# A hybrid attention / mLSTM trunk: the order of its instructions taken from a planner written into the kernel, with its own layout of the PSUM banks

## The chip, the cores and the metric

The kernel runs on one core of a Trainium2 chip. The metric is the device time of one execution in microseconds (us), the median of three runs. The chip's engines are called TensorE (matmuls), VectorE, ScalarE, GpSimd and SyncE here, and PE, DVE, ACT, POOL and SP in the profile; PEld is TensorE's loading of weights.

## The reference

One inference step of a trunk with two layers, for 512 sample tokens and 128 prompt tokens of 1024 features, in float32. Cut to what matters:

```
for l in range(2):
    shift, scale, gate = split(silu(c) @ W_mod[l] + b_mod[l])
    h = rmsnorm(x) * (1 + scale) + shift
    proj = h @ W_in[l]                       # 1024 x 5840
    o_a = latent attention, 4 heads          # low-rank q and kv, a shared rotary key
    o_b = differential attention, 4 heads    # two softmax maps a head, rmsnorm
    o_c = mLSTM, 4 heads, both directions    # gates -> scans -> per-chunk matmuls
    y = concat(o_a * silu(z_a), o_b * silu(z_b), o_c * silu(z_c)) @ W_out[l]
    x = x + gate * y
y_sample, y_prompt = rmsnorm(x) * g_final
```

Outputs are also the caches and the final mLSTM states of the prompt.

## The kernel before

The 640 tokens are five tiles of 128. Every large product is exact to nearly float32: each operand is split into a high and a low part (`hi`, `lo`), and `mm3` (L288 to L290) makes three matmuls of it. A weight section is loaded by SP into one of three `raw` slots, ScalarE casts the high part (L279), VectorE or, for each third section, GpSimd subtracts to get the low part (L282); both go to five slots of `fixr`. `tm_unit` gives token-major projections (tiles `tm`), `fm_unit` feature-major ones (`fm`), `out_proj` and `out_tail` the output projections (`op`), which VectorE multiplies by the gate (L538), GpSimd adds to the residual (L539), and a DMA of the ACT queue writes back (L540).

A layer runs the mLSTM branch (`gates`, then `mlstm_head` four times), differential attention (`diff_head`), latent attention (`mla_prep`, `mla_head`), each a chain of dependent steps. `Feed` holds the independent work (projections, the next layer's modulation) and is asked for a portion of it at each step of a chain, so that the program text already alternates chain and independent work. The Tile framework then orders each engine's instructions by a timeline of its own (`schedule_with_timeline_sim=True`). `issue_after` keeps the first layer's first section behind the modulation weights on SP.

Tiles of PSUM have three tags: `pj` (projections, 2 buffers of one bank), `sm` (small, 3), `S` (two banks each, 2: scores, transposes). The framework gives them banks as they come free, so that a projection may stand in a bank that a transposed tile has just left. Long-lived SBUF tiles share 35 slots of tag `Q`.

Names used below: `ds` scores of differential attention (L921, L922), made from `ksh`/`kp` and `ksl` (the high and low keys, L813 on ScalarE and L816 on VectorE) after the transposes `pkd` (L892); `pa` the transposes of the gate columns (L696), which need `gta` (L678) at the end of the scans `gb`, `edge`, `gta`, `gm` on VectorE; `as` scores of latent attention (L1149); `oT` transposes of a head's output (L513); `po` the product with the values (L831); `xT` transposes of the normalised tokens (L434); `sz` the SiLU of a gate path (L496); `msc`, a DRAM tile through which the row `gm` is spread over the partitions as `mb`.

Of the kernel before, what the change touches and what calls it, by code (L numbers as in the profile page):

```python
# [65 lines left out]
def parameter_columns(I):  # L66
    """Vectors of the inputs laid out as columns of 128, and the gate biases and stabilisers on their gate rows."""
# [12 lines left out]
class Feed:  # L80
    """Independent work, emitted in portions between the steps of a dependent chain."""
# [39 lines left out]

@with_exitstack
def tile_hybrid(ctx: ExitStack, tc: tile.TileContext, I: dict, O: dict):
    nc = tc.nc
    V, A, G, T = nc.vector, nc.scalar, nc.gpsimd, nc.tensor
# [3 lines left out]
    pp = ctx.enter_context(tc.tile_pool(name="pp", bufs=1, space=PSUM))  # L129
    dr = ctx.enter_context(tc.tile_pool(name="dr", bufs=1, space=DRAM))  # L130

    # independent work of a layer, in the order in which it fills the gaps of the dependent chains
# [7 lines left out]
    class Fixed:  # L140
        """One tile from which all that stays in its place is cut."""
# [14 lines left out]
    class Ring:  # L156
        """Slots used in turn, for tiles that live for a short stretch of the program."""
# [14 lines left out]
    def qt(name, dt=F32, n=TOK):  # L172
        return sb.tile([P, 645], dt, tag="Q", bufs=NQ, name=name)[:, 0:n]
# [7 lines left out]
    def pj(name):  # L181
        return pp.tile([P, 512], F32, tag="pj", bufs=2, name=name)

    def sm(name):
        return pp.tile([P, 512], F32, tag="sm", bufs=3, name=name)

    def s2(name):
        return pp.tile([P, 1024], F32, tag="S", bufs=2, name=name)

    # ---------------------------------------------------------------- constants and parameters  # L190
    A.preload_act_table_set("exp_and_others")
    con = fix.tile([P, C_END])
    nc.sync.dma_start(out=con[:, 0:C_RC], in_=I["consts"][:, 0:C_RC])
# [9 lines left out]
    # silu(cond) as stationary columns: [c_hi, ctx_hi, c_lo, ctx_lo] per k  # L203
# [13 lines left out]
    # half conv weights; norm gains with the half of z's silu  # L217
# [7 lines left out]
    def more_params():  # L225
        nc.sync.dma_start(out=con[:, C_RC:], in_=I["consts"][:, C_RC:])
# [6 lines left out]
    def lambdas(l):  # L233
        dl = qt("dl")
        nc.sync.dma_start(out=dl[:, 0:256],
# [11 lines left out]
    # ---------------------------------------------------------------- helpers  # L247
# [125 lines left out]
    def gate_tile(l, hf):  # L373
        """The residual gates of half of the features for the sample and for the prompt, on all partitions."""
        gs = [qt("gate", n=512) for _ in range(2)]
        for w in range(2):
            nc.sync.dma_start(out=gs[w], in_=grow[l][w:w + 1, hf * 512:(hf + 1) * 512].to_broadcast([P, 512]))
# [987 lines left out]
```

## Time and profile before

| | us |
|---|---|
| median of 3 runs | 1403.42 (1402.33 to 1403.47) |
| the profiled execution, first to last instruction (its span) | 1399.6 |
| TensorE matmul busy | 1310.0 (94%) |
| VectorE busy | 842.5 (60%) |
| ScalarE busy | 630.2 (45%) |
| GpSimd busy | 385.5 (28%) |
| DMA, mean rate | 112 GB/s |

The profiled execution is one of its own: its span is 1399.6 us, and what a run takes around the span is in the runs' 1403.42 us but not in it. Busy time of TensorE is that of pipelined matmuls whose ends are modelled, so 94% is not 94% of its peak; it is the time in which it had a matmul in hand.

### The profile page before, as it was taken

To read this page: it belongs to the slowest core of one execution; us is meant where nothing else is said; L and a number is where in the kernel's file an instruction comes from. 1 tells how busy PE (TensorE), PEld (TensorE's weight loads), DVE (VectorE), ACT (ScalarE), POOL (GpSimd) and SP (SyncE) were. 2 spreads that over 40 slices of the span, in tenths; PEclk is the share of its full clock that TensorE was granted. 3 is DMA by queue.
4 is the path that set the end of the run, shared out by engine and by line. 5 is a ranking of instruction groups with operands and counts; after the bars stand their busy time and mean duration, and the time that the engine had idled before them with its cause. 6 is when DMAs were issued, how large, how long until landed. Compare 5 with 4: busy or idle time off the path is not lost.

```text
span 1399.6 us, 24039 instructions
## 1 busy us (share of the span) xinstructions
PE 1310.0 (94%) x9300; PEld 1218.9 (87%) x9300; DVE 842.5 (60%) x1786; ACT 630.2 (45%) x1333; POOL 385.5 (28%) x335
## 2 busy tenths in 40 slices
PE   8989999989899999999979899999999999899995
PEld 3789899969899999798769899998799999878984
DVE  2576757765567465854465767675655646385446
ACT  5454544433455545255365345443343445435433
POOL 0421422323223013511432213333322202161142
PEclk9999999999999999999989999999999999999998
DMA  9423323264223223531751333434521211242154
GB/s 341 116 83 101 111 84 112 85 212 136 81 83 111 61 62 113 167 109 54 238 176 31 84 112 86 117 82 129 180 84 57 74 46 63 87 138 85 54 173 150
DMA packets 164642, 156.40 MB, mean 112 GB/s; under 512 B 14193, under 2 KB 130593, under 8 KB 164529
## 3 DMA queue, kind: packets, MB, share of 16 engines
q1 hardware_dynamic: 154032, 135.92, 32.0%
q10 hardware_dynamic: 10496, 18.95, 3.6%
q8 instruction: 73, 1.20, 0.3%
q14 instruction: 41, 0.33, 0.1%
HBM read 131.38 MB, written 23.46 MB: 111 GB/s over the span
## 4 chain that ended last, share of the span: by engine, by line
PE 73%; DVE 12%; DMA 5%; ACT 4%; issue 2%; POOL 2%; SPq 1%; DVEq 0%; ACTq 0%; POOLq 0%
PE tm L288 8%; PE tm L289 8%; PE tm L290 8%; PE fm L288 6%; PE fm L290 6%; PE fm L289 6%; PE po L831 5%; PE op L288 2%; PE pT L826 2%; PE op L289 2%; PE op L290 2%; DVE fixr L282 1%; PE nd L767 1%; PE ds L921 1%; DVE ksl L816 1%
## 5 line engine op out<-in xcount | busy, mean ns | idle before, releaser
L288 PE MATMUL tm<-fixr 128*128 128x256 f32 (+2 forms) x1040 | 302.0, 291 | 12.4 <-DVE kp L816 4.8
L289 PE MATMUL tm<-fixr 128*128 128x256 f32 (+2 forms) x1040 | 299.4, 288 | 0.2 <-DVE fixr L282 0.2
L290 PE MATMUL tm<-fixr 128*128 128x256 f32 (+2 forms) x1040 | 297.0, 287 | 2.5 <-DVE fixr L427 2.2
L282 POOL TENSOR_TENSOR fixr<-fix,fixr 128x1024 fp32r<-128x1024 f32 (+4 forms) x51 | 121.4, 2380 | 385.0 <-ACT fixr L279 365.4
L279 ACT CAST fixr<-fix 128x1024 fp32r<-128x1024 f32 (+2 forms) x154 | 157.8, 1030 | 128.7 <-PE fm L289 38.4
L288 PEld LDWEIGHTS tm<-fixr 128*128 128x128 f32 x1040 | 201.0, 193 | 15.3 <-issue 4.7
L290 PEld LDWEIGHTS tm<-fixr 128*128 128x128 f32 x1040 | 200.3, 193 | 3.0 <-DVE fixr L427 2.4
L289 PEld LDWEIGHTS tm<-fixr 128*128 128x128 f32 x1040 | 201.0, 193 | 1.4 <-issue 0.9
L288 PE MATMUL fm<-fixr 128*128 128x320 f32 x640 | 201.3, 314 | 0.5 <-ACT od L940 0.5
L290 PE MATMUL fm<-fixr 128*128 128x320 f32 x640 | 199.3, 311 | 0.0
L289 PE MATMUL fm<-fixr 128*128 128x320 f32 x640 | 198.6, 310 | 0.0
L282 DVE TENSOR_TENSOR fixr<-fix,fixr 128x1024 fp32r<-128x1024 f32 (+3 forms) x103 | 141.6, 1377 | 66.8 <-ACT fixr L279 62.3
L288 PEld LDWEIGHTS fm<-fixr 128*128 128x128 f32 x640 | 120.3, 188 | 2.2 <-ACT od L940 0.8
L290 PEld LDWEIGHTS fm<-fixr 128*128 128x128 f32 x640 | 120.2, 188 | 0.9 <-issue 0.9
L289 PEld LDWEIGHTS fm<-fixr 128*128 128x128 f32 x640 | 120.4, 188 | 0.0
L539 POOL TENSOR_TENSOR xp<-xp,ytmp 128x512 f32<-128x512 f32 x60 | 79.1, 1329 | 107.7 <-DVE ytmp L538 58.4
L288 PE MATMUL op<-fixr,oTh 128*128 128x512 f32 x240 | 100.5, 419 | 2.9 <-ACT oTh L516 1.7
L289 PE MATMUL op<-fixr,oTh 128*128 128x512 f32 x240 | 96.7, 403 | 0.0
L290 PE MATMUL op<-fixr,oTl 128*128 128x512 f32 x240 | 95.0, 403 | 0.0
L929 ACT ACTIVATE P<-ds,fix 128x640 f32<-128x640 f32 (+1 forms) x80 | 56.7, 709 | 72.7 <-DVE fix L928 70.4
L927 DVE TENSOR_REDUCE fix<-ds 128x1 f32<-128x640 f32 (+1 forms) x80 | 56.8, 713 | 47.4 <-PE ds L922 31.0
L252 POOL TENSOR_TENSOR fix<-fix 128x5 f32<-128x5 f32 (+1 forms) x31 | 31.6, 1019 | 130.4 <-DVE fix L251 129.9
(325 smaller groups left out, 2722.2 us busy)
## 6 DMA issues: line engine op xcount, KB each, us to landing
fix<-in_W_in SPq DMA_DIRECT2D x56, 512.0 KB, 4.2
fix<-in_W_mod SPq DMA_DIRECT2D x35, 512.0 KB, 4.3
fix<-in_W_in SPq DMA_DIRECT2D x64, 256.0 KB, 3.3
xd<-xp ACTq DMA_DIRECT2D x60, 256.0 KB, 2.5
xp<-xd SPq DMA_DIRECT2D x50, 256.0 KB, 4.4
fix<-in_W_out SPq DMA_DIRECT2D x24, 512.0 KB, 5.0
gate<-grow SPq DMA_DIRECT2D x32, 256.0 KB, 5.0
wm<-in_W_mod SPq DMA_DIRECT2D x26, 256.0 KB, 5.9
```

Of the source, the lines that this page charges most:

```text
L252: G.tensor_tensor(r[:, :n], a[:, :n], mhalf[:, :n], op=ALU.pow)
L279: A.copy(hv, rv)
L282: e.tensor_tensor(lv, rv, hv.bitcast(F32), op=ALU.subtract)
L288: T.matmul(ps, lhsT=wh, rhs=xh, start=start, stop=False)
L289: T.matmul(ps, lhsT=wh, rhs=xl, start=False, stop=False)
L290: T.matmul(ps, lhsT=wl, rhs=xh, start=False, stop=stop)
L539: G.tensor_tensor(xt, xt, y, op=ALU.add)
L767: T.matmul(nd[:, d, 0:129], lhsT=e[:, d], rhs=va[:, c, :], start=True, stop=(c == 4))
L826: T.transpose(ps[:, c * P:(c + 1) * P], pe[:, c * P:(c + 1) * P], idt)
L831: T.matmul(po[:, 0:P], lhsT=pt[:, c * P:(c + 1) * P], rhs=v3[:, c] if t < 4 else vp[:, hs], start=(c == 0), stop=(c == n - 1))
L927: V.tensor_reduce(sc[:, m:m + 1], pv, axis=ax, op=ALU.max, negate=True)
L929: A.activation(ev, pv, AF.Exp, scale=DIFF_SCALE, bias=sc[:, 2 + m:3 + m], accum_out=sc[:, 4 + m:5 + m])
```

## The change

Nothing of the arithmetic changes. Every call on an engine is recorded instead of issued (`Plan.Engine`, `Plan.add`); `link` finds which operation needs which by the parts of the tiles that they touch; `simulate` runs the list on a model of the five queues, each engine taking of its ready operations the one that was recorded first; `issue` then emits all operations in the order of their modelled starts, inside `tc.manual_schedule()`, so that the framework's own ordering is off and only its semaphores stay. Four things come with it:

- The model's durations are written out in `cost`, from the form of the operation alone. It has no ACT table loads, and a VectorE operation costs the same whatever GpSimd does.
- A tile of a tag can only start when all tiles of that tag recorded earlier have started (`rank`, `nxt`), and only `CAPS` of them live at once: 3 `pj`, 3 `sm`, 2 `S`, 35 `Q`.
- PSUM is one tile of eight banks. `S` has the pairs (0, 1) and (2, 3); `pj` takes banks 4 to 7 from below, `sm` the same four from above.
- All DMAs go through SP, also the 96 of the ACT queue before (write-backs of the residual, `msc`, gate rows). `issue_after` is gone.

```diff
+class Plan:
+    CAPS = {"pj": 3, "sm": 3, "S": 2, "Q": 35}
+    BANKS = {"pj": ((4,), (5,), (6,), (7,)), "sm": ((7,), (6,), (5,), (4,)), "S": ((0, 1), (2, 3))}
...
+    def cost(self, o):
+        m, e, k = o["m"], o["eng"], o["k"]
+        if m == "dma_start":
+            out = o["outs"][0]
+            return 350, 0, 4 * self.free(out) * int(out.shape[0])
+        if e == "PE":
+            if m == "transpose":
+                return 109, 273 + 45, 0
+            n = self.free(k["rhs"])
+            if "float32r" in str(k["rhs"].dtype):
+                return max(107, 0.4535 * n + 3), 175 + 0.4535 * n + 45, 0
+            return 2 * max(111, 0.845 * n), 280 + max(0, 0.845 * n * 2 - 110) + 45, 0
...
+        if e == "ACT":
+            t = 155 + 0.85 * n + (100 if ptr else 0) + (193 if "accum_out" in k else 0)
+            return t - 80, t + 45, 0
+        if e == "DVE":
+            t = 145 + 1.06 * n
+            if m == "tensor_copy" and not psum or m == "memset":
+                t = 145 + 0.53 * n
...
+            return t - 70, t + 45, 0
...
+    def simulate(self, prio):
...
+        def may(o):
+            for x in o["tiles"]:
+                if x not in have:
+                    tag = self.tags[x][0]
+                    if rank[x] != nxt[tag] or live[tag] >= self.CAPS[tag]:
+                        return False
+                    if tag in self.BANKS and not any(vacant.issuperset(b) for b in self.BANKS[tag]):
+                        return False
+            return True
...
+                    if o["bytes"]:
+                        dma = max(t + 1400, dma) + o["bytes"] / 230.0
+                        fin = dma + 600
...
+    def issue(self, tc):
+        self.link()
+        prio = [o["prio"] for o in self.ops]
+        start, end = self.simulate(prio)
...
+        with tc.manual_schedule():
+            for i in sorted(range(len(self.ops)), key=lambda i: (start[i], i)):
+                o = self.ops[i]
+                o["f"](*[place(x) for x in o["a"]], **{k: place(x) for k, x in o["k"].items()})
...
-                A.dma_start(out=xd[v][t][:, cs], in_=xt)
+                SP.dma_start(out=xd[v][t][:, cs], in_=xt)
...
-        with tc.issue_after(first[0].ins):
-            feed.need(("va", 0))
+        feed.need(("va", 0))
```

Three places show what this does to the order. In the rows of the change every line is L426, the line that emits, and every PSUM tile is `banks`.

TensorE at the first scores of differential attention, layer 0. Before, `pkd` are the key transposes, and eighteen matmuls `op` stand between the last of them and the first `ds`:

```order
L892 MATMUL pkd_2969<-fix_66,qkp_2702 128x128 x2
...
L289 MATMUL op_3018<-fixr_67,oTh_2916 128x512
L290 MATMUL op_3018<-fixr_67,oTl_2917 128x512
L921 MATMUL ds_3037<-ksh_2977,qs_2930 128x320
L922 MATMUL ds_3037<-ksl_2978,qs_2930 128x320
...
L921 MATMUL ds_3065<-ksh_2979,qs_2931 128x320
L922 MATMUL ds_3065<-ksl_2980,qs_2931 128x320
```

In the change:

```order
L426 MATMUL banks_64<-fixr_68,oTl_385 128x512
L426 MATMUL banks_64<-ksh_398,qs_388 128x320 x2
L426 MATMUL banks_64<-fixr_68,oTh_253 128x512 x2
L426 MATMUL banks_64<-fixr_68,oTl_254 128x512
L426 MATMUL banks_64<-fixr_68,oTh_297 128x512 x2
L426 MATMUL banks_64<-fixr_68,oTl_298 128x512
L426 MATMUL banks_64<-fixr_68,oTh_340 128x512
L426 MATMUL banks_64<-ksl_399,qs_388 128x320 x2
L426 MATMUL banks_64<-fixr_68,oTh_340 128x512
L426 MATMUL banks_64<-fixr_68,oTl_341 128x512
L426 MATMUL banks_64<-fixr_68,oTh_384 128x512 x2
```

Twenty-four `op` matmuls now stand between the last `pkd` and the first `ds`, seven more (a further output tile) between the `ds` that needs only high keys and the one that needs `ksl`, and five more before the second map.

VectorE in the gates of layer 0, between the second half of a convolution (`cvt`) and the running maxima (`gm`). Before:

```order
L616 SCALAR_TENSOR_TENSOR cvt_611<-up_610,fix_66,cvt_611 128x127
L643 SCALAR_TENSOR_TENSOR gb_640<-fix_66,ga_639 32x128
...
L618 SCALAR_TENSOR_TENSOR cvt_611<-up_610,cvt_611 128x640
...
L648 COPY edge_644<-gb_640 32x3
L649 COPY edge_644<-gb_640 32x3
L282 TENSOR_TENSOR fixr_67<-fix_66,fixr_67 128x1024
L647 TENSOR_TENSOR gta_641<-g_600,gb_640 64x640
L615 SCALAR_TENSOR_TENSOR cvt_684<-up_683,fix_66,cvt_684 128x511
L651 SCALAR_TENSOR_TENSOR gm_643<-edge_644,fix_66,gta_641 32x512
```

In the change:

```order
L426 SCALAR_TENSOR_TENSOR cvt_187<-up_186,fix_67,cvt_187 128x127
L426 SCALAR_TENSOR_TENSOR cvt_187<-up_186,cvt_187 128x640
L426 SCALAR_TENSOR_TENSOR gb_190<-fix_67,ga_189 32x128 x10
L426 COPY edge_194<-gb_190 32x3
L426 TENSOR_TENSOR gta_191<-g_185,gb_190 64x640
L426 COPY edge_194<-gb_190 32x3
L426 SCALAR_TENSOR_TENSOR gm_193<-edge_194,fix_67,gta_191 32x512 x2
```

The weight split (L282) and one convolution step have left the stretch; the convolution's last step (which needs ScalarE's tanh) now stands ahead of all ten scans `gb` instead of in their middle.

The transfers of `msc`. Before, on ScalarE's queue, between its other work:

```order
L612 ACTIVATE cvt_684<-fm_725,fix_66 128x320
L663 DMA msc0_757<-gm_643 4x640
L595 ACTIVATE mo_774<-tm_776 128x128
L595 ACTIVATE mo_775<-tm_776 128x128
L663 DMA msc0_757<-gm_643 4x640
```

In the change, on SP's queue, between its loads:

```order
L426 DMA fix_67<-in_W_in 128x8x128
L426 DMA msc0_200<-gm_193 4x640
L426 DMA out_new_mlstm_m<-gtb_192 4x1 x2
L426 DMA msc0_200<-gm_193 4x640
L426 DMA mb_211<-msc0_200 128x640
```

ScalarE no longer stands behind `gm`; SP does, and with it the loads that are queued there.

## Rows read from the trace of the kernel before

**Rows 1.** The page, part 1: engine busy us (share of the span) xinstructions.

```profile
PE 1310.0 (94%) x9300; PEld 1218.9 (87%) x9300; DVE 842.5 (60%) x1786; ACT 630.2 (45%) x1333; POOL 385.5 (28%) x335
```

**Rows 2.** Timeline of PE, the last matmul: start us, us, engine, line, op.

```profile
1385.63 0.40 PE L290 MATMUL op<-fixr,oTl 128*128 128x512 f32 x1
```

**Rows 3.** Waits of PE, longest total first: us in total, times, longest us.

```profile
PE as L1149 <- DVE fix L1162: 8.7, 6, 1.6
PE pa L696 <- DVE gta L678: 7.4, 2, 3.7
PE xT L434 <- ACT xs L410: 7.3, 3, 3.1
PE ds L922 <- DVE ksl L816: 6.0, 2, 3.9
PE tm L288 <- DVE kp L816: 4.8, 3, 2.5
PE ds L921 <- DVE kp L816: 4.5, 2, 2.3
PE po L831 <- ACT PT L828: 4.4, 6, 1.7
PE tm L288 <- DVE sz L496: 3.0, 1, 3.0
PE oT L513 <- DVE od L507: 2.3, 1, 2.3
```

**Rows 4.** Windows, five: length, busy (x) of PE PEld DVE ACT POOL, PEclk, DMA.

```profile
293.10:300.00 6.90, 4.60 (x14) 3.70 (x14) 5.30 (x12) 1.53 (x3) 2.52 (x2) 0.52 0.52 196
...
sum 31.30, PE 23.55 PEld 20.76 DVE 20.33 ACT 6.03 POOL 10.86; mean PE 4.71 PEld 4.15 DVE 4.07 ACT 1.21 POOL 2.17
```

**Rows 5.** Windows, three more stretches of half clock.

```profile
95.10:98.70 3.60, 3.21 (x15) 3.21 (x16) 1.92 (x8) 0.93 (x5) 0.46 (x1) 0.55 0.62 154
...
sum 21.00, PE 17.29 PEld 16.20 DVE 10.44 ACT 12.85 POOL 9.01; mean PE 5.76 PEld 5.40 DVE 3.48 ACT 4.28 POOL 3.00
```

**Rows 6.** Timeline of PE at the first scores of differential attention; [idle before <-releaser].

```profile
288.21 0.40 PE L290 MATMUL op<-fixr,oTl 128*128 128x512 f32 x1
288.44 0.31 PE L921 MATMUL ds<-ksh,qs 128*128 128x320 f32 x1
292.67 0.41 PE L922 MATMUL ds<-ksl,qs 128*128 128x320 f32 x1 [3.92 <-DVE ksl L816]
```

**Rows 7.** Timeline of DVE and PE at a projection behind a SiLU, 367 to 371.

```profile
367.47 2.73 DVE L282 TENSOR_TENSOR fixr<-fix,fixr 128x1024 fp32r<-128x1024 f32 x1
370.77 0.58 PE L288 MATMUL tm<-fixr 128*128 128x256 f32 x1 [3.05 <-DVE sz L496]
```

**Rows 8.** Timeline of DVE, POOL and ACT in the gates of layer 0.

```profile
83.34 2.39 POOL L282 TENSOR_TENSOR fixr<-fix,fixr 128x1024 fp32r<-128x1024 f32 x1 [13.38 <-ACT fixr L279]
83.49 2.26 DVE L648 COPY edge<-gb 32x3 f32<-32x3 f32 x1
85.78 0.16 DVE L649 COPY edge<-gb 32x3 f32<-32x3 f32 x1
92.10 0.28 ACT L595 ACTIVATE mo<-tm 128x128 f32<-128x128 f32 x1 [8.09 <-DVE gm L657]
```

**Rows 9.** Groups by form: xcount | busy us, mean ns | idle before <-releasers.

```profile
L282 DVE TENSOR_TENSOR fixr<-fix,fixr 128x1024 fp32r<-128x1024 f32 x94 | 129.1, 1375 | 59.8 <-ACT fixr L279 55.3 <-issue 2.3 <-PE pkd L892 1.3
L282 POOL TENSOR_TENSOR fixr<-fix,fixr 128x1024 fp32r<-128x1024 f32 x46 | 112.2, 2439 | 354.2 <-ACT fixr L279 334.6 <-ACT od L940 11.7 <-ACT fix L746 5.5
...
L560 DVE TENSOR_TENSOR xs<-xs,ytmp 128x512 f32<-128x512 f32 x10 | 12.2, 1222 | 0.1
L997 DVE TENSOR_TENSOR cq<-cq,fix 128x640 f32<-128x640 f32 x6 | 10.1, 1716 | 1.6 <-POOL fix L252 1.6
...
L637 ACT ACT_TABLE_LOAD x2 | 2.6, 1283 | 0.0
L617 ACT ACT_TABLE_LOAD x2 | 2.6, 1283 | 4.1 <-DVE cvt L616 4.1
```

More of the change, by code (lines that the diff above doesn't have):

```diff
@@ L124, in tile_hybrid @@
     nc = tc.nc
-    V, A, G, T = nc.vector, nc.scalar, nc.gpsimd, nc.tensor
+    plan = Plan()
+    V, A, G, T, SP = [plan.Engine(plan, n, e) for n, e in (("DVE", nc.vector), ("ACT", nc.scalar), ("POOL", nc.gpsimd),
+                                                        ("PE", nc.tensor), ("SP", nc.sync))]
     cst = ctx.enter_context(tc.tile_pool(name="cst", bufs=1))
@@ L129, in tile_hybrid @@
     pp = ctx.enter_context(tc.tile_pool(name="pp", bufs=1, space=PSUM))
+    plan.psum = pp.tile([P, 4096], F32, name="banks")
     dr = ctx.enter_context(tc.tile_pool(name="dr", bufs=1, space=DRAM))
@@ L172, in qt @@
     def qt(name, dt=F32, n=TOK):
-        return sb.tile([P, 645], dt, tag="Q", bufs=NQ, name=name)[:, 0:n]
+        return plan.tile("Q", sb.tile([P, 645], dt, tag="Q", bufs=NQ, name=name))[:, 0:n]
     def et(name):
@@ L181, in pj @@
     def pj(name):
-        return pp.tile([P, 512], F32, tag="pj", bufs=2, name=name)
+        return plan.tile("pj", pp.tile([P, 512], F32, tag="pj", bufs=2, name=name))
     def sm(name):
-        return pp.tile([P, 512], F32, tag="sm", bufs=3, name=name)
+        return plan.tile("sm", pp.tile([P, 512], F32, tag="sm", bufs=3, name=name))
     def s2(name):
-        return pp.tile([P, 1024], F32, tag="S", bufs=2, name=name)
-    A.preload_act_table_set("exp_and_others")
+        return plan.tile("S", pp.tile([P, 1024], F32, tag="S", bufs=2, name=name))
+    nc.scalar.preload_act_table_set("exp_and_others")
     con = fix.tile([P, C_END])
-    nc.sync.dma_start(out=con[:, 0:C_RC], in_=I["consts"][:, 0:C_RC])
+    SP.dma_start(out=con[:, 0:C_RC], in_=I["consts"][:, 0:C_RC])
     prm = con[:, C_PRM:C_RC]
@@ L293, in tile_hybrid @@
     wmod = I["W_mod"].rearrange("l (k p) n -> l p k n", p=P)
-    first = [None]
     def mod_rows(l, c0, pool):
@@ L376, in gate_tile @@
         for w in range(2):
-            nc.sync.dma_start(out=gs[w], in_=grow[l][w:w + 1, hf * 512:(hf + 1) * 512].to_broadcast([P, 512]))
+            SP.dma_start(out=gs[w], in_=grow[l][w:w + 1, hf * 512:(hf + 1) * 512].to_broadcast([P, 512]))
         return gs
@@ L530, in out_proj @@
                 xt = qt("xp", n=512)
[L531 removed]
+                SP.dma_start(out=xt, in_=x_src(v - 1, t)[:, cs])
                 ps = pj("op")
@@ L561, in tile_ @@
                 if l + 1 < DEPTH:
-                    A.dma_start(out=xd[v][t][:, cs], in_=xs[hf])
+                    SP.dma_start(out=xd[v][t][:, cs], in_=xs[hf])
             return xs
@@ L1326, in tile_hybrid @@
         hT = nxt_mods.get("hT")
+    plan.issue(tc)
 _INS = ["x_prompt", "x_sample", "cache_mla_ckv", "cache_mla_krope", "cache_diff_k", "cache_diff_v",
```

295 lines of the change are left out of this document (265 added, 30 removed).

## The prediction

> **What bounds the kernel now.** I read the page first: TensorE holds a matmul for 1310.0 of the 1399.6 us of the span, no other engine is near that [rows 1]. Then the end of TensorE's timeline: the last matmul ends at 1385.63 + 0.40 = 1386.03, so 13.6 us follow in which only the residual is finished [rows 2]. What lies between the matmuls is 1399.6 − 1310.0 − 13.6 = 76 us. The order of instructions can win only that, and what is lost when TensorE's clock falls; the number of matmuls stays.
>
> The view of waits says where the 76 us are [rows 3]: the scores of latent attention (`as`, 8.7), the gate columns (`pa`, 7.4), the transposes at a layer's edge (`xT`, 7.3), the scores of differential attention (`ds`, 6.0 behind the low keys and 4.5 behind the high ones), projections that wait for keys or for a SiLU (4.8 and 3.0), the product with the values (`po`, 4.4), a branch's last transposes (`oT`, 2.3). All are short, and each stands where a chain of VectorE or ScalarE steps outlasts the matmuls put beside it.
>
> The windows show a second price. After waits of some 2 to 4 us the granted clock stands near a half: five such stretches have 23.55 us of busy TensorE at 0.50 to 0.54, of which half, 11.8 us, is lost [rows 4]; three more have 17.29, that is 8.6 us [rows 5]. So a wait of 4 us that turns into matmuls saves more than itself.
>
> **The change, part by part.** The matmuls and their shapes are the same, so PE's 1310.0 changes only by the clock. I take each wait group and ask what matmuls the new order puts into it.
>
> *A, `ds`.* Before, TensorE has run out of `op` matmuls: the first `ds` starts at 288.44, the next, which needs `ksl`, 3.92 us idle later [rows 6]. A 512-column matmul is issued each 288.44 − 288.21 = 0.23 us [rows 6]. The new order has 24 instead of 18 such matmuls ahead of the first `ds` (6 × 0.23 = 1.4 us), 7 behind it (1.6) and 5 more before the second map (1.2): 4.2 us of work where 3.9 + 2.4 were idle. Layer 1 gains as many. Of the 10.5 us [rows 3] I take 9; the bounds are 2 × 4.2 = 8.4 and all 10.5.
>
> *B, projections that wait for a bank.* A `tm` matmul does not read `kp` or `sz`. It waits because its output tile was given a bank that VectorE was still reading: at 367 a split of 2.73 us stands on VectorE, and the projection starts 3.05 us late, released by `sz` [rows 7]. In the change, projections have banks 4 to 7, with `sm` coming from the other end, and a third buffer. Transposed tiles of tag `S` can no longer be in their way, `sm` tiles can. 4.8 + 3.0 = 7.8 [rows 3]; I take 7, bounds 0 (the third `pj` meets `sm`) and 7.8.
>
> *C, `pa`.* The matmuls that stand between the gate transposes and `pa` grow little (from 21.0 to 22.7 us of issue in layer 0, 21.3 to 22.4 in layer 1, counted in the order at 0.23 us for each 512 columns and as many per column for others: an estimate). 1.7 + 1.1 = 2.8. On VectorE a weight split leaves the chain (1.4, the mean of [rows 9]), but the convolution's last step comes ahead of all scans and waits for ScalarE's tanh. I take 4 of the 7.4, bounds 0 and 7.4.
>
> *D, `oT`, and E, `po`.* More `op` and projection matmuls lie between a head's last step and its `oT`, and one or two between each `P` and its `po`. I take 3 for D (2.3, and a little of the waits of the next tile behind it) and 2 of the 4.4 for E, bounds 0 and 3, 0 and 4.4.
>
> *F, `as`.* Before, several `as` follow `oT` directly; now five matmuls stand between. These last about 1 us, the waits are 8.7 / 6 = 1.5 us each [rows 3]: I take 4, bounds 0 and 8.7.
>
> *G, `xT`.* The layer's edge stays a chain of norm, split, transposes with nothing independent left: 1 of 7.3, bounds 0 and 3. The end behind the last matmul stays too.
>
> *H, half clock.* The five stretches of [rows 4] follow waits of A, B and D and a `tm` wait like B. If these waits shrink below what was seen ahead of a fall, 11.8 us come back; the three of [rows 5] follow `pa` and `xT`, which stay. I take 11, bounds 3 and 20.4 (all eight).
>
> *I, the move of DMAs to SP.* Before, ScalarE stood still for 8.09 us behind a transfer that needed `gm` [rows 8]; now SP stands there. Behind it in SP's queue are loads of weights. With three `raw` slots SP asks for a section up to two sections ahead, and one of 512 columns keeps TensorE for 5 tiles × 8 × 3 matmuls × 0.23 = 28 us [rows 6], so that lead covers the wait; were it gone, the next cast of a section, and the projection behind it, would come up to 8 us late. ScalarE's 8 us were off TensorE's path, except in so far as `pa` hides behind them. I count 0, bounds 0 and +8 (one such wait that reaches TensorE).
>
> *J, what the model of the planner leaves out.* An order made on wrong durations is late where the real step is longer. Its price for the VectorE split is 145 + 1.06 × 1024 = 1.23 us, against a mean of 1.375 in 94 of them: 129.1 − 94 × 1.23 = 13.5 us [rows 9]. `xs` is priced at 0.688 against 1.22 (12.2 − 10 × 0.688 = 5.3), `cq` at 0.823 against 1.72 (10.1 − 6 × 0.823 = 5.2), and it knows no ACT table loads (4 × 1.28 = 5.1) [rows 9]. The sum is 29 us on engines that are busy 60% and 45% [rows 1]. Most of it falls where there is slack; I take a fifth, +6, bounds 0 and 29.
>
> The rows show where the first of these comes from: a VectorE copy of 3 elements takes 2.26 us while GpSimd works on a split from 83.34 to 85.73, and 0.16 us just behind it [rows 8]. The planner has no such effect. [...]
>
> Sum: −9 −7 −4 −3 −2 −4 −1 = −30 for waits, −11 for the clock, 0 for SP, +6 for the model's errors: −35. 1399.6 − 35 = 1364.6 for the span. The median of the runs lies 1403.42 − 1399.6 = 3.8 us above the profiled span; with that, **1368 us**.
>
> **The rivals.** *R2, nearly everything goes.* The planner fills each hole; the 48 us of waits in the nine groups of [rows 3] shrink by three quarters (−36), the others, 76 − 48 = 28, by half (−14), both sums of half clock return (−20), and the model's errors cost 2: −68, 1335. For it: no chain in the trace is longer than the independent work of its layer. Against it: `xT` and the first 4 us have no work to fill them.
>
> *R3, no measurable change.* The program text already interleaves; the new order differs by a few matmuls at each place, and a wait removed at one shows up at the next, as when `ksl` is in time and the next step, `P`, is late. If A and B alone win (−14, and −5 of clock) and J's share reaches 16 to 20, the time is 1399 to 1404. For it: the cover at `pa` grows by only 1 to 2 us.
>
> *R4, slower: the order is made for a VectorE that is never blocked.* A split on GpSimd takes 2.44 us, and there are 46 [rows 9]. A VectorE step that comes at a chance moment in one waits half of it, 1.2 us: 46 × 1.2 = 56 us, beside J's 29, so 85 us of delay that the model doesn't see, in an order that cannot give way (the order before was not made for it either, but its waits are those of the trace). The gain without J is 41 us; the change becomes slower when more than 41 + 3 of the 85 reach TensorE, a half. At two thirds: 57 − 41 = +16, 1419. For it: the blocked copy stands in the very chain that `pa` waits for. Against it: a good part of that 56 us is in the trace of before as well, and VectorE's idle time is 40% of the span.
>
> **How the numbers follow.** My forecast, 1352 to 1390 (the sum with J at 0 and H at 20, or with B, C and F at a half and J at 15), has 0.55. R2 has 0.18, R3 0.12, R4 0.15. A measurement here can tell 0.2% from no change, that is 2.8 us, 1400.6 to 1406.2. Faster holds the forecast, R2 and half of R3: 0.55 + 0.18 + 0.06 = 0.79; same the other half of R3 and a little of R4, 0.07; slower the rest of R4, 0.14. The range leaves out the lower half of R2 and most of R4: 1336 to 1402.
>
> **What the profile after would show.** A: no wait of over 1 us behind `ksl` or `kp`, and granted clock 1.0 through both starts of differential attention. B: no projection released by a VectorE step that it doesn't read. C: `pa` waits of 1 to 3 us, still the largest single ones besides `xT`. H: two to four stretches near 0.5 instead of the eight of [rows 4, 5]. J and R4: if I am wrong on the slow side, TensorE's waits are many and short, released by VectorE steps that lie beside a GpSimd split, and the VectorE split's mean is above 1.375 us. If I am wrong on the fast side, `as` and `po` have gone from the list of waits. PE's busy time should fall from 1310.0 by about the 11 us of the clock; were it unchanged, H would be wrong, whatever the end.

## The result and the profile after

The change makes the kernel slower: 1412.73 us median (1412.18 to 1413.42), against 1402.88 (1401.62 to 1403.47) of the kernel before in the same runs; the ratio is 1.0074, with a 95% interval of 1.0059 to 1.0088. I had forecast 1368 and given "slower" 0.14.

The page of the profile, part 1, after (busy us, share of the span, instructions), and the last rows of TensorE's timeline:

```profile
span 1410.9 us, 23957 instructions
PE 1313.6 (93%) x9300; PEld 1213.7 (86%) x9300; DVE 832.6 (59%) x1786; ACT 634.2 (45%) x1333; POOL 384.6 (27%) x335
```

```profile
1394.72 0.40 PE L426 MATMUL banks<-fixr,oTl 128*128 128x512 f32 x1
```

The span is 11.3 us longer than that of [rows 1]'s execution, and it splits like the forecast's sum. TensorE is busy for 3.6 us more (I had 11 less, by the clock). After the last matmul, which ends at 1395.1, 15.8 us are left instead of 13.6. The idle time between matmuls is 1410.9 − 1313.6 − 15.8 = 81.5 us where it was 76: I had forecast 30 less, and 6 us on top for the planner's errors.

The view of TensorE's waits after (us in total, times, longest). All lines are L426, so groups go by the tile waited for:

```profile
PE banks L426 <- DVE gta L426: 11.3, 2, 5.7
PE banks L426 <- DVE fix L426: 7.9, 7, 4.4
PE banks L426 <- DVE ytmp L426: 6.7, 5, 2.4
PE banks L426 <- ACT xs L426: 6.6, 2, 4.2
PE banks L426 <- ACT Pa L426: 6.6, 5, 1.6
PE banks L426 <- DVE hs L426: 6.0, 5, 2.0
PE banks L426 <- DVE fixr L426: 5.3, 6, 1.3
PE banks L426 <- ACT PT L426: 3.6, 5, 0.8
PE banks L426 <- ACT fixr L426: 3.5, 1, 3.5
...
PE banks L426 <- DVE sz L426: 2.6, 3, 1.8
...
PE banks L426 <- DVE ksl L426: 0.8, 2, 0.6
...
PE banks L426 <- DVE kp L426: 0.6, 1, 0.6
```

Against [rows 3]: the waits on `ksl` and `kp` are nearly gone (15.3 to 1.4 us). In their place stand longer waits on `gta` (7.4 to 11.3) and waits on `hs` (6.0), on `ytmp` (6.7), and on a ScalarE cast at the very head (3.5). Four places show what happened.

**First, differential attention is as predicted.** TensorE at the first scores, where [rows 6] had 3.92 us idle (start us, us, then the instruction):

```profile
301.35 0.39 PE L426 MATMUL banks<-fixr,oTl 128*128 128x512 f32 x1
301.58 0.46 PE L426 MATMUL banks<-ksh,qs 128*128 128x320 f32 x2
301.87 0.63 PE L426 MATMUL banks<-fixr,oTh 128*128 128x512 f32 x2
...
303.27 0.39 PE L426 MATMUL banks<-fixr,oTh 128*128 128x512 f32 x1
303.50 0.45 PE L426 MATMUL banks<-ksl,qs 128*128 128x320 f32 x2
```

No wait, and the granted clock is 1.00 from 300 to 310 us, where it was 0.52 at this place before [rows 4].

**Second, the head.** The windows from 20 to 40 us, before and then after (length, busy (x) of PE PEld DVE ACT POOL, PEclk, DMA, GB/s):

```profile
20.00:30.00 10.00, 9.05 (x49) 3.73 (x49) 5.31 (x14) 7.50 (x17) 1.18 (x1) 1.00 1.09 365
30.00:40.00 10.00, 10.00 (x57) 5.41 (x57) 4.96 (x9) 4.09 (x6) 4.16 (x3) 1.00 1.09 340
```

```profile
20.00:30.00 10.00, 5.86 (x23) 3.07 (x24) 3.07 (x8) 6.36 (x17) 0.35 (x1) 0.59 1.09 372
30.00:40.00 10.00, 9.28 (x36) 3.45 (x35) 3.70 (x9) 4.86 (x8) 2.00 (x2) 0.73 1.00 290
```

TensorE issues 59 matmuls in these 20 us instead of 106. Its granted clock falls to near a half (0.59 and 0.73 in these windows, 0.52 from 22 to 36 us) beside a wait of 3.54 us, up to 23.34, on a cast of the modulation weights:

```profile
23.34 0.37 PE L426 MATMUL banks<-fixr 128*4 128x256 f32 x1 [3.54 <-ACT fixr L426]
```

```profile
18.78 0.36 ACT L426 COPY fix<-banks 4x256 f32<-4x256 f32 x1 [2.11 <-PE banks L426]
...
22.69 1.12 ACT L426 CAST fixr<-fix 128x512 fp32r<-128x512 f32 x2
```

On ScalarE that cast (22.69; before, 19.58) stands behind eight of the ten square sums of the tokens, five of them after a copy that waits 2.11 us for TensorE. Before, it stood behind seven, which began earlier. The planner prices a DMA at 230 bytes a ns, and so believes that the weights come later than they do (365 and 340 GB/s in the windows of before); `e_dma` below shows how much of the wait comes from that (3.54 us fall to 2.04).

**Third, the gates.** TensorE at `pa`, then GpSimd and VectorE at one scan, and ScalarE's two table loads:

```profile
94.83 2.30 PE L426 MATMUL banks<-fixr 128*128 128x256 f32 x18
102.81 1.33 PE L426 MATMUL banks<-fix,gta 128*128 128x128 f32 x5 [5.68 <-DVE gta L426]
```

```profile
88.19 0.41 DVE L426 TENSOR_TENSOR_SCAN gb<-fix,ga 32x128 f32<-32x128 f32 x1
89.05 2.99 DVE L426 TENSOR_TENSOR_SCAN gb<-fix,ga 32x128 f32<-32x128 f32 x2
89.37 2.39 POOL L426 TENSOR_TENSOR fixr<-fix,fixr 128x1024 fp32r<-128x1024 f32 x1 [12.90 <-ACT fixr L426]
```

```profile
79.47 1.28 ACT L426 ACT_TABLE_LOAD   x1
...
84.54 1.28 ACT L426 ACT_TABLE_LOAD   x1 [2.05 <-DVE cvt L426]
```

A scan takes 0.41 us; of the pair at 89.05 one takes over 2 us more, and the pair ends at 92.04, 0.28 us behind the GpSimd split (89.37 + 2.39 = 91.76). The planner knows neither this nor the loads (1.28 us each), and `pa` starts 5.68 us late. How much of that each of them makes is asked below.

**Fourth, the end of an mLSTM head** (DVE, POOL and PE):

```profile
287.18 3.00 DVE L426 TENSOR_TENSOR hs<-hs,fix 128x640 f32<-128x640 f32 x1 [1.28 <-POOL fix L426]
287.12 2.38 POOL L426 TENSOR_TENSOR fixr<-fix,fixr 128x1024 fp32r<-128x1024 f32 x1
290.24 0.55 PE L426 MATMUL banks<-fix,hs 128*128 128x128 f32 x3 [1.45 <-DVE hs L426]
```

A step that takes 0.82 us elsewhere starts 0.06 us behind a GpSimd split and takes 3.00, that is until the split ends (289.50) and 0.68 more; the transposes `oT` wait 1.45 us for it. Of the five waits of the group `hs` (6.0 us) two stand behind such a blocked step (1.45 and 1.98); the three others follow steps of 0.82 us, so a block of this step does not explain them. The same step is blocked once in the trace of before, beside a GpSimd split from 275.90 to 278.31:

```profile
276.19 2.80 DVE L507 TENSOR_TENSOR hs<-hs,fix 128x640 f32<-128x640 f32 x1
```

There no wait of TensorE follows: other matmuls (the next layer's modulation, then `op`) fill the time until `oT` starts at 279.22.

Over the whole trace of the change, VectorE instructions take 69 us more than others of their form do (78 us in the trace of before), always beside a GpSimd instruction (all 77 that took over 0.1 us more than the shortest of their form, and all 100 in the trace of before). Of those that started while a GpSimd elementwise operation had 0.3 us or more to run, 73 of 84 with SBUF operands alone (elementwise with two tensors, scans, casts) were stretched by over 0.1 us, 69 of them until it ended and their own time beyond; of 253 others (an operand in PSUM, reductions, reciprocals, tensor-scalar steps) none was. The tensor-scalar steps among these from SBUF are all of 128x1; in the trace of before three of 128x5 took 0.33, 0.72 and 1.28 us instead of 0.17 beside a GpSimd instruction. What these counts show is called the exclusion below.

### The profile page after: what moved, and what is told of

Its sections match the earlier page's. It is cut to its first block, busy times and chain, and to the rows that moved or that the text cites. A ratio compares the mean times of both kernels' runs of the same rounds, so it can differ in the third digit from the quotient of the medians.

```text
span 1410.9 us, 23957 instructions
## 1 busy us (share of the span) xinstructions
PE 1313.6 (93%) x9300; PEld 1213.7 (86%) x9300; DVE 832.6 (59%) x1786; ACT 634.2 (45%) x1333; POOL 384.6 (27%) x335
## 4 chain that ended last, share of the span: by engine, by line
PE 69%; DVE 14%; issue 6%; ACT 5%; POOL 3%; DMA 3%; DVEq 0%; SPq 0%; POOLq 0%; ACTq 0%
PE banks L426 69%; DVE fix L426 3%; DVE fixr L426 2%; DVE cvt L426 2%; ACT fixr L426 1%; POOL fix L426 1%; DVE ksl L426 1%; DVE xs L426 1%; DVE ytmp L426 1%; DMA wm<-in_W_mod 1%; ACT ksh L426 1%; DVE gb L426 1%; DMA fix<-in_W_in 1%; POOL fixr L426 1%; DVE hs L426 1%
## 5 line engine op out<-in xcount | busy, mean ns | idle before, releaser
L426 PE MATMUL banks<-fixr 128*128 128x256 f32 (+6 forms) x5732 | 827.5, 298 | 26.3 <-ACT Pa L426 6.6
L426 PEld LDWEIGHTS banks<-fixr 128*128 128x128 f32 (+1 forms) x5732 | 757.7, 185 | 48.9 <-ACT Pa L426 7.7
L426 POOL TENSOR_TENSOR fixr<-fix,fixr 128x1024 fp32r<-128x1024 f32 (+4 forms) x51 | 120.3, 2358 | 386.4 <-ACT fixr L426 386.4
L426 ACT CAST fixr<-fix 128x1024 fp32r<-128x1024 f32 (+6 forms) x164 | 164.0, 1008 | 93.8 <-PE banks L426 61.3
L426 DVE TENSOR_TENSOR fixr<-fix,fixr 128x1024 fp32r<-128x1024 f32 (+5 forms) x114 | 150.1, 1321 | 64.4 <-ACT fixr L426 64.0
L426 PE MATMUL banks<-fixr,oTh 128*128 128x512 f32 x480 | 156.7, 406 | 5.3 <-DVE ytmp L426 2.9
L426 DVE TENSOR_REDUCE fix<-banks 128x1 f32<-128x640 f32 (+1 forms) x120 | 84.8, 714 | 76.2 <-PE banks L426 73.0
L426 PEld LDWEIGHTS banks<-fixr,oTh 128*128 128x128 f32 x480 | 87.3, 190 | 23.9 <-DVE ytmp L426 4.6
L426 POOL TENSOR_TENSOR xp<-xp,ytmp 128x512 f32<-128x512 f32 x60 | 82.1, 1381 | 88.7 <-DVE ytmp L426 39.5
L426 PE MATMUL banks<-fixr,oTl 128*128 128x512 f32 x240 | 95.6, 402 | 0.1
L426 ACT ACTIVATE P<-banks,fix 128x640 f32<-128x640 f32 (+1 forms) x80 | 56.6, 709 | 83.1 <-DVE fix L426 77.9
L426 DVE TENSOR_TENSOR ytmp<-banks,gate 128x512 f32<-128x512 f32 x80 | 54.3, 687 | 40.9 <-PE banks L426 27.1
L426 POOL TENSOR_TENSOR fix<-fix 128x5 f32<-128x5 f32 (+1 forms) x31 | 32.5, 1049 | 145.7 <-DVE fix L426 145.6
L426 ACT ACTIVATE fix<-mb,fix 128x128 f32<-128x128 f32 x144 | 50.3, 397 | 23.7 <-DMA mb<-msc 8.7
L426 POOL TENSOR_TENSOR mb<-mb,fix 128x128 f32<-128x128 f32 x80 | 41.9, 548 | 63.1 <-DMA mb<-msc 32.0
L426 PEld LDWEIGHTS banks<-fixr,oTl 128*128 128x128 f32 x240 | 45.3, 190 | 10.6 <-POOL oTl L426 1.0
L426 ACT COPY PT<-banks 128x640 f32<-128x640 f32 (+1 forms) x80 | 48.0, 605 | 12.9 <-PE banks L426 10.8
L426 POOL TENSOR_TENSOR qk<-qk,fix 128x256 f32<-128x256 f32 x32 | 24.4, 764 | 89.3 <-DVE fix L426 82.7
L426 DVE RECIPROCAL fix<-fix 128x2 f32<-128x2 f32 (+1 forms) x120 | 19.5, 163 | 49.1 <-ACT P L426 24.4
L426 DVE TENSOR_TENSOR fix<-banks,fix 128x128 f32<-128x128 f32 (+3 forms) x144 | 31.3, 240 | 26.8 <-PE banks L426 25.7
L426 ACT ACTIVATE Pa<-banks,fix 128x640 f32<-128x640 f32 (+1 forms) x40 | 28.4, 709 | 39.9 <-DVE fix L426 35.5
L426 DVE SCALAR_TENSOR_TENSOR cvt<-up,fix,cvt 128x511 f32<-128x511 f32 (+1 forms) x64 | 40.5, 662 | 7.8 <-ACT cvt L426 7.8
```

Source lines behind the costliest of these rows:

```text
L426: o["f"](*[place(x) for x in o["a"]], **{k: place(x) for k, x in o["k"].items()})
```

## The experiments

Ratios are to the kernel before, with 95% intervals; the change has 1.0074.

### The planner's DMA rate, and the hold at the head

`e_dma`:

```diff
-                        dma = max(t + 1400, dma) + o["bytes"] / 230.0
+                        dma = max(t + 1400, dma) + o["bytes"] / 370.0
```

> The change with one number of its planner altered: a DMA moves 370 instead of 230 bytes a ns, as the first 40 us of the trace show (340 to 396 GB/s). Theory (the order of ScalarE at the head comes from a planner that expects the modulation weights too late): the casts of these weights stand ahead of most square sums again, TensorE's 3.5 us wait at 20 us and the stretch of half clock from 22 to 36 us go, the work that was done at 57.5 us is done at about 50, and the time falls by 6 to 9 us, to 1404 to 1407. Rival (the head is late because W_in now goes ahead of the last modulation weights on SP, which this edit leaves): the head stays as late, 1410 to 1414.

Measured: 1.0028 [1.0012, 1.0043], at the slow end of the theory. TensorE's wait on the cast falls from 3.54 to 2.04 us, and 86 matmuls stand in the 20 us where the change has 59. The order of ScalarE is not what the theory said: the cast still stands behind eight square sums, only these begin at 12.19 instead of 14.45 us. A new wait of 2.6 us on a modulation weight's DMA follows at 40 us. `e_hold` adds the hold, as a rule of the planner:

```diff
         def may(o):
+            if o.get("hold") is not None and o["hold"] not in begun:
+                return False
```

where `hold` of the first eight loads of `W_in` is the last load of the modulation weights of layer 0.

> The change with the DMA rate of 370 bytes a ns, as before, and the hold of the first layer's first section behind the last modulation weights on SP put back (the planner does not start these eight loads before). The edit of the rate alone won some 4 of the 8 us that TensorE is late at 57 us. Theory (the other 4 are the hold that the change took away): the matmuls that stand at 49 us in the trace of before stand at 49 to 51 again, and the ratio to before falls from 1.0028 to 0.999 to 1.001. Rival (the rest of the head is ScalarE's order of casts and square sums, or half clock): no further gain, 1.002 to 1.004.

Measured: 1.0033 [1.0020, 1.0045], the same as without the hold. The windows of `e_hold`:

```profile
20.00:30.00 10.00, 7.99 (x39) 3.89 (x40) 5.15 (x13) 7.75 (x17) 1.19 (x1) 0.83 1.09 370
30.00:40.00 10.00, 10.00 (x61) 5.80 (x60) 4.42 (x9) 3.38 (x6) 1.56 (x2) 1.00 0.96 287
```

At the head itself the two together work: 100 matmuls now, where the change has 59. The rate is worth some 0.4%; of what the hold wins there, nothing is left at the end, and the theory of the hold falls as far as the total goes.

### The exclusion of VectorE and GpSimd: told to the planner, and taken away

`e_lock` tells the planner of the exclusion, for forms like those stretched in the trace of the change (73 of 84; it also keeps the matmul groups of one PSUM tile in their recorded order, an edit that `e_margin` and the versions under Together have too; it moves next to nothing in the planner's list; no run has it alone, but `c_headbank`, which has it, shows no gain of its own from it):

```diff
+            o["port"] = o["eng"] == "POOL" or (o["eng"] == "DVE" and not psum and o["m"] in (
+                "tensor_tensor", "scalar_tensor_tensor", "tensor_tensor_scan", "tensor_copy"))
...
+            if o["port"] and port[1] != o["eng"] and port[0] > t:
+                return False
```

> The change with a planner that knows one more thing: a VectorE operation on SBUF operands alone (elementwise with two tensors, scan, copy) and a GpSimd operation do not run at once. Theory (the order suffers from VectorE steps that stand behind a GpSimd operation): stretched VectorE time falls from 69 us to under 30, TensorE's waits behind such steps (oT, pT, ckT, krT, part of pa; together some 12 us) mostly go, and the time falls by 8 to 14 us, to 1399 to 1405. Rival (the blocks only move: the same GpSimd work must be done, and an order that keeps off it pays the same in waiting): 1410 to 1416, with the stretched time down all the same.

`e_nopool` takes the weight splits off GpSimd instead, and `b_nopool` does the same to the kernel before:

```diff
-            e = G if pool and cnt[0] % pool == 0 else V
+            e = V
```

> The change with every weight split on VectorE, none on GpSimd (the 51 that GpSimd did cost VectorE some 62 us more). Theory of the blocks: stretched VectorE time falls to under 30 us without any change of the planner, so TensorE waits less behind it, but VectorE has more to do: net -5, 1404 to 1412. Rival (VectorE's own load decides, the blocks do not): VectorE's chains become longer by a split here and there, 1418 to 1432.

> The kernel before with every weight split on VectorE, none on GpSimd. The same edit won 1.3% on the change. Theory A (the order of before stands beside the GpSimd splits in a way that costs TensorE little, though it has as much stretched VectorE time, 78 us): no gain, ratio 0.997 to 1.004, so that the blocks are what sets the change apart. Theory B (the blocks cost TensorE in both orders alike): ratio 0.985 to 0.993, so that they do not explain why the change is slower than before.

Measured: `e_lock` 0.9934 [0.9919, 0.9949], `e_nopool` 0.9942 [0.9926, 0.9957], `b_nopool` 0.9952 [0.9940, 0.9965]. Both edits win about 1.3% on the change, more than their theories gave (8 to 14 us, and about 5 net), and either is enough to make it faster than before. In `e_nopool` the waits that stood behind splits shrink, `hs` from 6.0 to 1.4 us and `gta` from 11.3 to 7.1:

```profile
PE 1311.1 (94%) x9300; PEld 1214.0 (87%) x9300; DVE 846.3 (61%) x1837; ACT 634.1 (45%) x1333; POOL 270.5 (19%) x284
```

```profile
PE banks L426 <- DVE gta L426: 7.1, 2, 3.5
...
PE banks L426 <- DVE hs L426: 1.4, 2, 0.7
```

VectorE has 51 more splits, which should be some 62 us (an estimate: 51 times the 1.21 us of the group's mean in `e_nopool`), and is busy for only 14 us more than in the change (846.3 against 832.6); most of the difference is that the stretched time fell from 69 to 29 us. In `e_lock` no wait on `hs` is left among TensorE's groups, but the stretched time fell to 53 us only, where the theory had under 30. The planner lets no such pair overlap on its timeline, but the chip's times drift from it, and a split still falls on the ten scans ahead of `pa`. Here are the scans in the change, then those of `e_lock` with the split and the wait on `gta`, which is what it was:

```profile
87.35 6.40 DVE L426 TENSOR_TENSOR_SCAN gb<-fix,ga 32x128 f32<-32x128 f32 x10
```

```profile
90.75 6.40 DVE L441 TENSOR_TENSOR_SCAN gb<-fix,ga 32x128 f32<-32x128 f32 x10
92.78 2.39 POOL L441 TENSOR_TENSOR fixr<-fix,fixr 128x1024 fp32r<-128x1024 f32 x1 [13.34 <-ACT fixr L441]
```

```profile
PE banks L441 <- DVE gta L441: 11.3, 2, 5.7
```

`b_nopool` lies between its two theories: the kernel before gains too, but 0.5% against 1.3%, although its stretched time falls about as far (78 to 41 us). Without these splits the two kernels are alike (0.9942 and 0.9952, intervals that overlap). So the splits on GpSimd take from the change 0.8% more than from the kernel before, as much as the whole distance between the two. They are not the only thing that closes it: `e_margin` and `e_anybank` below do so with the splits in place.

### What makes `pa` late

`e_gates` ranks the gates' operations ahead of the convolution's:

```diff
-        feed.along(gates(l, R))
+        feed.along(ahead(gates(l, R)))
```

(`ahead` sets the recorded number of every operation of `gates` to that of the first.)

> The change with the steps of the gates ranked ahead of the convolution (their operations get the number of the first of them). On VectorE the four convolution steps (2.2 us) between the running maxima and the last step before pa move behind it. Theory Z (the planner puts pa exactly where it expects its input, so a shorter chain only moves pa up by as much, and the lateness that the planner does not know, table loads and a blocked scan, stays): pa comes some 17 matmuls earlier, the two waits of 5.7 us stay at 4.5 or more each, ratio 1.005 to 1.009. Rival (the convolution in the chain is the price at pa): the waits fall to 3.5 us or less each, 1.000 to 1.004.

Measured: 1.0078 [1.0061, 1.0095], no gain. `pa` comes 1.6 us earlier, and the waits are nearly the same (10.7 us in all, 11.3 in the change). The first of the two:

```profile
101.25 1.33 PE L426 MATMUL banks<-fix,gta 128*128 128x128 f32 x5 [5.25 <-DVE gta L426]
```

`e_table` tells the planner of the table loads (1283 ns ahead of a logarithm, and of the next tanh; the trace of before has two of 1283 ns at each of these, L637 and L617 [rows 9]):

```diff
+                        if fn.endswith("Ln") and fset[0] != "ln":
+                            fset[0], load = "ln", 1283
+                        elif fn.endswith("Tanh") and fset[0] == "ln":
+                            fset[0], load = "", 1283
```

> The change with a planner that knows the four ACT table loads of 1.28 us and nothing else. Theory (two loads lie in each gate chain, and the planner puts pa where it expects its input): pa's two waits fall from 5.7 by up to 2.6 us each, some of the half clock behind them goes, ratio 1.001 to 1.005. Rival (the loads are beside the chain, the blocked scan makes the lateness): 1.005 to 1.009, waits as before.

Measured: 1.0037 [1.0022, 1.0052], a gain of 0.4%; the two waits are 4.1 us each:

```profile
PE banks L434 <- DVE gta L434: 8.2, 2, 4.1
```

The first of these is the most telling run. A shorter chain won nothing: by its rule the planner starts `pa` as soon as it believes that `gta` is done, so `pa` moved up with `gta`, and the wait stayed. What each of the things that it doesn't know makes of this wait can be told in part. The loads known take 3.1 us off the 11.3, the splits off GpSimd 4.2, the exclusion known by itself nothing. `e_all`, with loads and exclusion known, still has 7.7; `c1`, which also has the gates ranked first, the hold and any bank, has 2.3:

```profile
PE banks L449 <- DVE gta L449: 7.7, 2, 3.9
```

```profile
PE banks L462 <- DVE gta L462: 2.3, 2, 1.2
```

No run tells which of these last three takes the 5.4 us between them.

### A margin at every step

`e_margin` tells the planner nothing true, only that results are seen 0.3 us later:

```diff
-                    heappush(ev, (fin, 1, i))
+                    heappush(ev, (fin + (0 if e == "PE" or o["bytes"] else 300), 1, i))
```

> The change with a planner that counts the result of each VectorE, ScalarE and GpSimd operation as seen 0.3 us later by the other engines, and otherwise believes the same durations. Theory Z (an order that puts each step where its input is expected has no room for what comes late): waits of TensorE behind these engines get fewer, ratio 0.990 to 1.001, without any effect modelled. Rival (only the right effects at the right places help; a margin at each step makes the order worse): 1.007 to 1.020.

Measured: 0.9978 [0.9962, 0.9995], a gain of 1.0% on the change. The waits on `gta` fall from 11.3 to 8.2 us and those on `hs` from 6.0 to 1.1, while those on `fix` and `ytmp` rise (7.9 to 12.2, 6.7 to 11.5). Room for lateness alone, at the wrong size and at each step alike, wins two thirds of what the exclusion wins, told rightly (1.4%).

### Banks, buffers, queue

`e_anybank` and `e_pj2`:

```diff
-    BANKS = {"pj": ((4,), (5,), (6,), (7,)), "sm": ((7,), (6,), (5,), (4,)), "S": ((0, 1), (2, 3))}
+    BANKS = {"pj": tuple((b,) for b in range(8)), "sm": tuple((b,) for b in range(7, -1, -1)), "S": ((0, 1), (2, 3), (4, 5), (6, 7))}
```

```diff
-    CAPS = {"pj": 3, "sm": 3, "S": 2, "Q": 35}
+    CAPS = {"pj": 2, "sm": 3, "S": 2, "Q": 35}
```

> The change with its layout of the PSUM banks undone: projections and small tiles may take any of the eight banks, scores any of four pairs, the planner's limits of 3, 3 and 2 tiles stay. Theory (the layout neither costs nor wins much; what is lost is lost to durations that the planner has wrong): ratio to before 1.004 to 1.011, as the change. Rival A (banks 4 to 7 for two tags bind): faster than the change by over 0.5%. Rival B (the layout holds off the waits on kp and sz that the change removed): slower than the change by 0.5% or more.

> The change with two projection tiles at once instead of three, as before. If the third buffer is what took the waits of projections on kp and sz away (7.8 us before, some 3 now), they come back and more, since the order has to wait for an eviction at each tile: ratio 1.013 to 1.025. Rival (the third buffer does nothing): 1.005 to 1.009.

Measured: `e_anybank` 0.9991 [0.9982, 1.0000], 0.8% faster than the change, so rival A; `e_pj2` 1.0369 [1.0349, 1.0389], worse than either theory. In `e_pj2` projections wait for the readers of their old tiles:

```profile
PE banks L426 <- DVE ytmp L426: 14.0, 11, 2.3
...
PE banks L426 <- DVE sz L426: 9.3, 6, 3.2
```

The third projection buffer is what this order lives on. The layout costs some 0.8% here, with the wait on `sz` falling from 2.6 to 0.6 us.

`e_actq` gives ScalarE's 96 transfers back to its queue, eight lines of this kind:

```diff
-                SP.dma_start(out=xd[v][t][:, cs], in_=xt)
+                A.dma_start(out=xd[v][t][:, cs], in_=xt)
```

> The change with the 96 transfers of ScalarE's queue back on it. Theory (their move to SP neither won nor cost): ratio 1.004 to 1.011. Rival A (SP stands behind them and the loads come late): faster than the change by 0.4% or more. Rival B (ScalarE was freed by the move): slower by 0.4% or more.

Measured: 1.0071 [1.0052, 1.0090], as the change: the move is worth nothing either way. The waits do change places: those on `gta` are 6.9 us instead of 11.3, and 3.8 us on ScalarE's `mo` are new.

### Together

`e_all` has the rate, the exclusion and the table loads; `c_headbank` the rate, the hold and any bank; `c1` all of these and the gates ahead; `c2` is `c1` with all weight splits on VectorE. Their diffs are those above.

> The change with a planner that has the DMA rate of 370 bytes a ns, the exclusion of VectorE and GpSimd, and 1.28 us for each of the four ACT table loads. Theory (what the planner leaves out is what the change costs): the sum of the two other edits and 2 to 4 us for the table loads, so 1412.7 less 16 to 27, 1386 to 1397, faster than before. Rival (the cause is in the order's rule, the ready operation that was recorded first, or in the banks): only the head is won, 1403 to 1408.

> The change with the DMA rate of 370 and the hold at the head and with any bank for any tag, nothing else: GpSimd splits and the planner's belief about them as in the change. If the head (the ratio fell by 0.4%) and the banks (by 0.8%) are parts of the loss of their own: 1.0074 less 1.2%, 0.993 to 0.998, faster than before without a word on the blocks. If each of the two gains was a chance of one order that another order gives back: 1.000 to 1.005.

> The version with all edits but one: a third of the weight splits stays on GpSimd, and the planner knows the exclusion. If the planner's knowledge is worth as much as taking the splits away (alone they gave 0.9934 and 0.9942): 0.978 to 0.984, as the version without the splits (0.9808). If GpSimd's splits cost by themselves, known or not: 0.985 to 0.991.

> All that helped together: the DMA rate of 370, the hold at the head, the exclusion of VectorE and GpSimd and the table loads in the planner, the gates ranked first, any bank for any tag, and all weight splits on VectorE. If the gains added up (head 6, blocks 18, banks 11): 1412.7 less 35, ratio about 0.982, 0.978 to 0.986. If they are one and the same slack, won once: 0.990 to 0.994, as the edits of the blocks alone.

Measured: `e_all` 0.9912 [0.9893, 0.9930]; `c_headbank` 1.0005 [0.9992, 1.0018]; `c1` 0.9827 [0.9808, 0.9847]; `c2` 0.9808 [0.9786, 0.9830], 1375.96 us against 1402.7 in the same runs, the fastest version and faster than both kernels. Its part 1, and its largest waits:

```profile
PE 1300.3 (95%) x9300; PEld 1208.8 (88%) x9300; DVE 841.1 (61%) x1837; ACT 631.8 (46%) x1333; POOL 272.3 (20%) x284
```

```profile
PE banks L462 <- DVE ytmp L462: 8.3, 8, 3.6
PE banks L462 <- DVE fixr L462: 6.7, 5, 4.3
PE banks L462 <- ACT xs L462: 6.3, 3, 2.9
```

The waits on `gta` and `hs` are gone from the list's top, and TensorE's busy time is 13 us lower than in the change. Its mean granted clock is 0.987 where the change has 0.978, which over 1373 us is some 12 of the 13, an estimate (0.009 × 1373).

`e_all`, `c1` and `c2` came out as their first theories said. `c_headbank` did not: it lies in the range of its rival, by which a gain can be a chance of one order that another gives back. Head and banks win 0.4 and 0.8% alone and 0.7% together. So single gains of half a per cent are not to be added up; two edits that were expected to move nothing, `e_gates` and `e_actq`, did stay within 0.1% of the change. `c1` beside `c_headbank` shows the larger part: with the exclusion, the loads and the gates' rank the version wins 1.8% more. And `c1` beside `c2` shows that the GpSimd splits may stay, as long as the planner knows them (0.2% apart, within the intervals).

## Why the prediction was wrong

The prediction said 1368, faster; it is slower by 0.7%. The step that failed is **J**, what the planner leaves out, at +6: too small a sum, and too small a share of it. The sum was 29 us, of which 24 come from three groups of VectorE steps; over the whole trace of before VectorE is stretched by 78 us. The share was a fifth. Taking the splits off GpSimd lets an estimate be made of it. In the change the stretched time fell by 40 us (69 to 29) and the time by 18 (1.0074 to 0.9942), nearly a half; in the kernel before it fell by 37 (78 to 41) and the time by 7 (to 0.9952), which is the fifth that I took. Both are net of the splits that VectorE then had to do.

The reason that the runs support is this: an order built on a model puts a dependent step where the model expects its input, so a lateness that the model does not know finds little room there. Told to the planner, the exclusion is worth 1.4% (some 20 us), the table loads 0.4% (some 5), the DMA rate 0.4 to 0.5% (some 6), all three 1.6% (22 us, `e_all`) in place of J's 6; and 0.3 us of room at each step, with nothing told, 1.0%.

J is not the whole miss of 45 us. Without it the forecast was 1362, and `e_all`, whose planner knows the three things, stands at 0.9912, some 1390. The 28 us between them are gains that didn't come. `c1` wins 12 of these by the gates' rank, the hold and any bank, and `c2` some 3 more; even `c2` has about 60 us of idle time between matmuls, where 76 − 30 = 46 were forecast. So the points below count beside J.

The rival R4 had the mechanism, with its place (the copy of [rows 8]; now a scan), and I gave it 0.15 because the trace of before has such blocks too. It has, and `b_nopool` shows that they cost it 0.5% where they cost the change 1.3%. But that R4's 1419 lies near the 1412.73 is in part luck: it needed 44 of its 85 us to turn the result, the exclusion and the loads known win back some 25, and the rest is gain that R4 took as won. That each of the 46 splits holds one VectorE step for half its length, R4's 56 us, was an estimate; no run shows this term. What the traces show is 78 us of stretched time in the trace of before, in 100 steps beside GpSimd instructions of all kinds, and 69 us in 77 steps in that of the change.

Point by point:

- **A** was right: the waits of the scores fell from 10.5 to 1.4 us; I took 9.
- **B** was right in kind: 7.8 to 3.2, I took 7. `e_pj2` shows that the third buffer does it. The layout, on which I had rested it as well, wins nothing and costs 0.3 to 0.8%.
- **C** was wrong in sign: 7.4 to 11.3. I counted the matmuls between the gate transposes and `pa` as cover. In a planned order cover is no stock: it is what the planner believes to be needed. `e_gates` shortened the chain, and the cover shrank with it. Loads and exclusion known leave 7.7 us, so a part of the lateness stays unexplained.
- **D** was wrong in sign for the mLSTM branch: the 2.3 us, which stood behind differential attention's `od`, fell to 1.4, but 6.0 us behind `hs` are new. 3.4 of them stand behind steps blocked by a split; `e_nopool` leaves 1.4 of the 6.0, and `e_lock` none.
- **E** and **F** were too high. `po` fell by 0.8 (I took 2). For `as`, the waits on `fix` and `Pa` fell together from 8.7 + 2.7 to at most 10.1 (the group of 7.9 holds one of 4.4 at the program's start): about 1 of the 4 I took.
- **G**: 7.3 to 6.6, as taken.
- **H** was wrong: of the five stretches of [rows 4] one is left, shorter, but the one at the head and three short ones are new. The mean granted clock of the whole span is 0.978 where it was 0.977, so the clock gave nothing back; why the busy time rose by 3.6 us is not shown. (The five windows of [rows 4] were granted 0.52 to 0.58, not 0.50 to 0.54, so a little under half of their time was lost: a 256-column matmul was issued each 0.21 us where the clock was half, each 0.12 elsewhere. Nor was every wait of this length followed by a fall: a wait of 2.36 us up to 172.09 in the trace of before was not, at 1.00 from 168 to 176.) The windows after, of the head and of the one that is left:

```profile
22.00:36.00 14.00, 11.13 (x38) 4.70 (x38) 5.14 (x13) 7.60 (x17) 1.19 (x1) 0.52 1.08 336
...
376.40:380.00 3.60, 3.60 (x18) 3.60 (x19) 1.96 (x5) 0.00 (x0) 1.17 (x1) 0.55 0.73 203
```

- **I** was right about the move (`e_actq`). No term stood for the head. By 40 us TensorE is 47 matmuls behind there; the rate told gives back 27 of these and the hold 14 more, which together are worth 0.4% of the total.
- The new waits on `ytmp` (6.7 us) I did not foresee: `op` tiles wait for VectorE to read the last one, in `c2` as well (8.3).
- The bounds of the range were added up wrong: by their own terms 1353 to 1385, not 1352 to 1390. It changes nothing here.

Open is why the hold's gain at the head does not reach the end, why head and banks together win less than the sum, and what else the planner has wrong at `pa`. Each edit makes the planner lay out all that follows anew, and a few waits of 1 to 3 us fall differently; I have not tried to hold the later order fixed.

## What to carry to other kernels

An order computed from a model leaves little room where the model is sure, so more of its error reaches the end (by the estimate above nearly a half, where the order of before let through a fifth): list first what the model does not know (here the stretched VectorE steps, 69 us in the change; four table loads of 1.28 us; DMAs at 340 to 396 GB/s from 10 to 40 us of the trace of before, against the model's 230) and compare its starts with a trace, before counting covered waits. Telling the model is not the same as being rid of the effect: with the exclusion told, a split still fell on the scans. Where the model cannot be mended, give it some room at each step; 0.3 us won 1% here. And when a profile shows an operation at several times its usual duration, look at what the other engines did in that time.

## What I had not expected of the hardware

That the exclusion is so regular: every one of VectorE's 77 stretched instructions in the change lay beside a GpSimd instruction, 69 of the 73 that began while it had 0.3 us or more to run took their own time behind it, and none of the 253 others (an operand in PSUM, reductions, reciprocals, tensor-scalar steps) was stretched. And its cost to engine time: moving 51 splits of 1.2 us from GpSimd to VectorE made VectorE busy for only 14 us more (832.6 to 846.3).
